# A decoder block on one Trainium2 core: the second delta-net chain keeps its convolved tiles in SBUF, reloads change queue, column sums and four x tiles are moved

## The chip, the cores and the metric

One core of one Trainium2 chip runs the whole block in one launch. The metric is the device time of that core in microseconds, the median over several runs. Engines are named as the profile does: PE (TensorE), DVE (VectorE), ACT (ScalarE), POOL (GpSimd) and SP (SyncE). SP, ACT and POOL can each start DMA transfers, and each does so from an in-order queue of its own instructions (SPq, ACTq, POOLq).

## The reference, cut to what matters

One layer on 512 tokens of width 2048, float32. A vector c gives six modulation rows through w_ada; two token mixers (latent attention and gated delta-net) read the same projection p; they are merged by sigmoid gates, and a SwiGLU mixer follows.

```python
mod = c_act @ w_ada[l] + b_ada[l]
sh_a, sc_a, gt_a, sh_f, sc_f, gt_f = [m[:, None, :] for m in jnp.split(mod, 6, axis=-1)]
h = _rmsnorm(x, norm_mix[l]) * (1.0 + sc_a) + sh_a
p = h @ w_in[l]
c_q, c_kv, k_pe, q_g, k_g, v_g, z, b_logit, a_logit, gate_logits = _split_cols(p)
y_a = _mla_branch(c_q, c_kv, k_pe, ...) @ w_o_mla[l]
qkv = jnp.concatenate([q_g, k_g, v_g], axis=-1)
y_b = _gdn_branch(qkv, z, b_logit, a_logit, ...) @ w_o_gdn[l]
g_a, g_b = jnp.split(jax.nn.sigmoid(gate_logits), 2, axis=-1)
mix = (g_a * y_a + g_b * y_b) @ w_o[l]
x = x + gt_a * mix
...
# _gdn_branch: 8 heads of 128
qkv = _causal_conv_silu(qkv, conv_w)        # width 4, along the tokens
q = _l2norm(q) * DK ** -0.5 ; k = _l2norm(k)
# _gated_delta_chunked, chunks of 64 tokens
A = Lmat + I                                # Lmat: strictly lower, k k^T with decay
u, w = triangular_solve(A, [v * beta, k * beta * exp(G)])
def step(S, inp):                           # scanned over the chunks
    v_new = u_c - w_c @ S
    o = (q_c * exp(G_c)) @ S + a_c @ v_new
    S = S * exp(G_last) + k_dec^T @ v_new
```

## The kernel before, in words

**Matmuls.** Each weight tile comes from HBM as float32 (`raw`, `raws`), is split into a rounded part `hi` (ACT) and a rest `lo` (DVE), and PE takes three products for one. A *unit* is 24 matmuls on 512 tokens, and PE runs the units of w_in, w_ukv, w_uq, w_o_mla, w_o_gdn, w_o, w_gate_up and w_down one behind the other. Stages are named by their PSUM tiles: v (551 to 612 us), gb0 to gb3 (the four groups of the second gate, 612 to 875), qpe, v0, v1, qk, ya, yb (1106 to 1193), then `m` of w_o in two halves of its width (1193 to 1270 and from there), and gate-up and down.

**Order.** The whole program is first recorded in a `Score`, then emitted. PE, POOL and SP keep the order in which the program recorded their instructions; for DVE and ACT a list scheduler (`Score.order`) chooses by due times. Generators (`Driver`) advance side work between the units: the delta-net chains, the attention, the column sums. All instructions are emitted in one place, so every row of the profile has the line L490; rows are told apart by tile names.

**SBUF.** 68 shared slots of 128 x 512 (`S(name)`) hold nearly every tile that lives for some time; 5 wide buffers hold raw weights. Weight loads are issued 4 ahead, splits 2 ahead.

**DMA helpers.** `load()` issues on SP, `side()` on POOL, `nc.scalar.dma_start` on ACT.

**The delta-net.** `conv_tile(idx, p)` convolves one of 24 tiles (idx 0 to 7 are the eight heads of q, 8 to 15 those of k, 16 to 23 those of v, in `cv_dram[0]` to `cv_dram[2]`; heads 0 to 3 of each belong to chain 0, 4 to 7 to chain 1), stores it in `cv_dram` and keeps some in `conv_out`. `gdn(g)` is a chain of four heads, g = 0 and 1: it turns q and k tiles on PE (`pq`, `pk`), builds L and the attention products, solves the triangular systems by blocks (`fsL`, `fsX` on DVE, stored in `fso`, reloaded as `T` tiles; `T64T`, `TT`, `M` join the blocks), and scans four chunks of 128 tokens with `vp`, `AT` and `kdec`, which it stored in `gdn_dram` and reloads by `back(c)`. `conv_back(j, g)` reloads four convolved tiles. `pause(ns)` holds a chain back until the planner's clock has moved so far.

**Column sums.** The modulation rows are sums over the rows of w_ada, and over w_in's gate columns for another term, in 160 *extras*: a 512-KB load and DVE work each (`rawm`, `rawa`). `PLAN` says how many extras go with a unit, by the unit's index: (n, r) means r per unit up to index n. Unit indexes: v stage 97 to 104, gb0 105 to 112, gb1 113 to 120, gb2 121 to 128, gb3 129 to 136, qpe 137 and 138, v0 and v1 139 to 142, qk 143 to 150, ya from 151, yb 171 to 190.

**w_o.** `X_AT` says before which unit (n, i) of w_o which x tiles (token tile, column tile) are loaded. In the second half, stored partial sums (`raws<-s_dram`) and a row of the gate (`row<-gm_dram`) are reloaded on the same SP queue; ACT's and DVE's `euvw` are combinations of weight tiles that PE's `m` takes as its operand.

Of the kernel before, what the change touches and what calls it, by code (L numbers as in the profile page):

```python
# [499 lines left out]
def block_kernel(ctx: ExitStack, tc: tile.TileContext, a: dict, out):  # L500
    score = Score(tc)
    nc = Core(score)
# [16 lines left out]
    def S(s, dt=F32):  # L519
        return slots.tile([P, 512], dt, tag="s", name=nm(s))  # L520
# [10 lines left out]
    def side(dst, src, **kw):  # L531
        nc.gpsimd.dma_start(dst, src, **kw)
# [3 lines left out]
    def tok(j):  # L536
        return slice(j * P, (j + 1) * P)
# [347 lines left out]
    conv_out = {}  # L885

    def conv_tile(idx, p):
        acc = S("cv")
        nc.scalar.activation(acc[:], p[:], AF.Copy, scale=cw[:, 72 + idx:73 + idx])
        for w in (2, 1, 0):  # L890
            sft = 3 - w
            nc.vector.scalar_tensor_tensor(acc[:, sft:], p[:, :T - sft], cw[:, 24 * w + idx:24 * w + idx + 1],
                                           acc[:, sft:], op0=ALU.mult, op1=ALU.add)
        nc.scalar.activation(acc[:], acc[:], AF.Silu)
        side(cv_dram[idx // 8, idx % 8], acc[:])
        conv_out[idx] = acc if idx in (0, 1, 2, 3, 8, 9, 10, 11) else None

    cv_dram = dram.tile([3, 8, P, 512], F32, name="cv_dram")

    def conv_back(j, g):  # L900
        res = []
        for i in range(4 * g, 4 * g + 4):
            x = S("cv")
            nc.scalar.dma_start(x[:], cv_dram[j, i])
            res.append(x)
        return res

# [8 lines left out]
    def conv_gen():  # L916
        while True:
            if conv_queue:
                conv_tile(*conv_queue.popleft())
            yield  # L920
# [165 lines left out]
    def pause(ns):  # L1086

        until_ = score.time + ns
        while score.time < until_:
            yield  # L1090

    gdn_dram = dram.tile([2, 3, NT, P, 512], F32, name="gdn_dram")
    mid = set()

    def gdn(g):
# [5 lines left out]
        def back(c):  # L1101
            res = []
            for j in (0, 1, 2) if c < NT - 1 else (0, 1):
                x = S(("vp", "AT", "kdec")[j])
                nc.scalar.dma_start(x[:], gdn_dram[g, j, c])
                res.append(x)
            return res

        def conved(*parts):
            while not all(8 * j + 4 * g + i in conv_out for j in parts for i in range(4)):  # L1110
                yield

        yield from conved(0, 1)
        while "eG" not in G or (g and "loops" not in mid):
            yield
        if g:
            kT, qT = conv_back(1, 1), conv_back(0, 1)
            yield 9
        else:
            qT, kT = ([conv_out.pop(b + i) for i in range(4)] for b in (0, 8))  # L1120
            yield 4
        yield from conved(2)
        while g and 0 not in mid:
            yield
        vT = conv_back(2, g)

        def tr4(src, c, name):
            ps = PS(name)
# [86 lines left out]
        for j in range(31):  # L1215
# [4 lines left out]
            nc.vector.tensor_tensor(fsX[:, j + 1:, 0:w], fsX[:, j + 1:, 0:w], tv, ALU.subtract)  # L1220
            if j % 8 == 7:
                yield
        yield from pause(34000.0)
        for hf in range(2):
            side(fso[g].rearrange("b c h i a -> (b c h) i a")[:, :, 16 * hf:16 * hf + 16], fsX[64 * hf:64 * hf + 64])
        del fsX_, fsX, fsT, fsL
# [2 lines left out]
        for b in range(4):  # L1229
            side(T32[32 * b:32 * b + 32, :].rearrange("p (n a) -> p n a", a=32),  # L1230
                                fso[g][b].rearrange("c h i a -> i (c h) a"))
        yield from pause(11000.0)
        while g and "second" not in mid:
            yield
        T64 = [S("T64"), S("T64")]
# [59 lines left out]
        while not (g or 1 in mid):  # L1295
            yield
        kT, qT, cur = conv_back(1, g), conv_back(0, g), back(0)
        yield 5
        for hf in range(2):
# [12 lines left out]
        for c in range(NT):  # L1312
# [3 lines left out]
            if c < NT - 1:  # L1316
                cur = back(c + 1)
# [458 lines left out]
    def mix_row(n):  # L1776
        g_mix[n] = S("row")
        load(g_mix[n][:], gm_dram[512 * n:512 * n + 512].partition_broadcast(P))

    def load_x(t, n, src):  # L1780
        x2[t, n] = S("x2")
        load(x2[t, n][:], src[:, 512 * n:512 * n + 512])
# [254 lines left out]
    def plan(i):  # L2037

        return next(r for n, r in PLAN if i < n)

    PLAN = ((17, 2.0), (33, 0.0), (89, 0.4), (97, 0.0), (113, 0.5), (137, 1.5), (143, 1.0), (156, 0.0), (175, 2.0), (1000, 1.5))

    cs_dram = dram.tile([D], F32, name="cs_dram")
    gparts = kpe[:, 0, :].rearrange("p (k j) -> p k j", j=4)
# [35 lines left out]
    def with_pre(units, fn):  # L2080
        u = units[0]
        p0 = u.pre

        def pre():
            fn()
            if p0 is not None:
                p0()
        u.pre = pre
        return units
# [137 lines left out]
    def mixing():  # L2227
# [73 lines left out]
        def start_gdn():  # L2301
            drv.ahead = LOADS
            for g in range(2):
                ch["AB"[g]] = drv.add(gdn(g))
                drv.add(gated_out(g))
# [43 lines left out]
        for n in range(4):  # L2349
            us = fm_set(f"yb{n}", lambda k0, nk, n=n: plain(w_og, k0, nk, 512 * n, 512), 512, 8, ov, yb_done(n))  # L2350
            if n == 0:
# [4 lines left out]
                with_pre(us, fin)  # L2356
            yield read_gates("b", n)
            yield from us
        X_AT = {(0, 12): ((0, 1),), (0, 14): ((1, 1),), (1, 0): ((2, 1),), (1, 1): ((3, 1), (0, 3)), (1, 2): ((0, 0), (1, 3)), (1, 3): ((1, 0), (0, 2)),
                (1, 4): ((2, 0), (1, 2)), (1, 5): ((3, 0), (2, 3)), (1, 6): ((3, 3),), (1, 7): ((2, 2), (3, 2))}  # L2360
        for n in range(2):
            us = tokens_wo(n)
            if n == 0:
# [9 lines left out]
            for i, u in enumerate(us):  # L2373
                if n == 0 and i in (12, 13):
                    with_pre([u], lambda i=i: mix_row(i - 12))
                if n and i in (4, 5):
                    with_pre([u], lambda i=i: mix_row(i - 2))
                if (n, i) in X_AT:
                    with_pre([u], lambda c=X_AT[n, i]: [load_x(t, f, a["x"][tok(t), :]) for t, f in c])
                if n and i == 16:  # L2380
# [878 lines left out]
    def everything():  # L3259
        yield from mixing()  # L3260
        yield from ffn()
# [58 lines left out]
```

## Time and profile before

| | |
|---|---|
| three runs | 2684.03, 2680.06, 2679.77 us, median 2680.06 |
| the profiled execution | 2676.04 us, its span 2674.3 us, mean granted clock 0.992 |
| busy time | PE 2642.3, DVE 2252.0, ACT 1298.1, POOL 250.0 us |
| moved by DMA | 649.00 MB, mean 243 GB/s |
| DMA issues from 600 to 900 us | `cv<-cv_dram` 28 on ACT, 256 KB, 5.4 us to landing; `vp` 8, `AT` 8, `kdec` 6 on ACT; `rawa` 32 and `raw` 27 on SP, 512 KB, 5.9 and 5.6 us |

The profile is one execution. A row of a timeline has the start, the duration, the engine or queue, the tiles written and read, and in brackets the time that the engine was idle before and what ended that. A row of the windows has each engine's busy time, then the granted TensorE clock as a share of full speed, then the DMA engines' mean busy share and the rate. A queue such as ACTq is the time that the engine's sequencer spends issuing transfers; while it does, later instructions of that engine stand behind.

### The profile page before, as it was taken

To read this page: it belongs to the slowest core of one execution; us is meant where nothing else is said; L and a number is where in the kernel's file an instruction comes from. 1 tells how busy PE (TensorE), PEld (TensorE's weight loads), DVE (VectorE), ACT (ScalarE), POOL (GpSimd) and SP (SyncE) were. 2 spreads that over 40 slices of the span, in tenths; PEclk is the share of its full clock that TensorE was granted. 3 is DMA by queue.
4 is the path that set the end of the run, shared out by engine and by line. 5 is a ranking of instruction groups with operands and counts; after the bars stand their busy time and mean duration, and the time that the engine had idled before them with its cause. 6 is when DMAs were issued, how large, how long until landed. Compare 5 with 4: busy or idle time off the path is not lost.

```text
span 2674.3 us, 36928 instructions
## 1 busy us (share of the span) xinstructions
PE 2642.3 (99%) x12652; PEld 2196.4 (82%) x12652; DVE 2252.0 (84%) x3447; ACT 1298.1 (49%) x2004; POOL 250.0 (9%) x427
## 2 busy tenths in 40 slices
PE   9999999999999999999999999999999999999998
PEld 7888888887787888888788888888888888888887
DVE  8988888888986878899897888888887888877888
ACT  4355444464444684235484444444444445444445
POOL 0000110132410000000100000000000001010000
PEclk9999999999998999999999999999999999999999
DMA  9985777886888738956864777776766668686785
GB/s 351 351 282 165 260 272 259 308 281 228 260 276 274 236 105 273 332 176 207 269 205 132 237 236 241 248 234 226 236 227 205 208 222 277 210 247 226 226 294 207
DMA packets 335540, 649.00 MB, mean 243 GB/s; under 512 B 48116, under 2 KB 77108, under 8 KB 335352
## 3 DMA queue, kind: packets, MB, share of 16 engines
q1 hardware_dynamic: 277624, 511.43, 58.0%
q0 software_dynamic: 29584, 94.18, 9.7%
q10 hardware_dynamic: 28144, 41.03, 4.5%
q8 instruction: 99, 1.62, 0.2%
q14 instruction: 89, 0.73, 0.1%
HBM read 537.95 MB, written 107.50 MB: 241 GB/s over the span
## 4 chain that ended last, share of the span: by engine, by line
PE 85%; DMA 6%; issue 4%; DVE 3%; ACT 1%; ACTq 0%; SPq 0%; POOL 0%; DVEq 0%; POOLq 0%
PE m L490 52%; PE v L490 4%; PE gu L490 3%; PE ya L490 3%; PE ga L490 3%; PE yb L490 3%; PE s L490 3%; PE gb L490 2%; PE dn L490 2%; PE qk L490 2%; PE dnt L490 2%; DMA rawa<-in_w_in_dram 1%; PE sc L490 1%; DMA raws<-in_w_down_dram 1%; DMA raw<-in_w_in_dram 1%
## 5 line engine op out<-in xcount | busy, mean ns | idle before, releaser
L490 ACT CAST hi<-raws 128x512 fp32r<-128x512 f32 (+1 forms) x472 | 430.5, 915 | 666.1 <-PE m L490 338.1
L490 DVE TENSOR_TENSOR lo<-raws,hi 128x512 fp32r<-128x512 f32 (+1 forms) x472 | 487.9, 1051 | 153.8 <-ACT hi L490 148.2
L490 ACT CAST hi<-raw 128x1024 fp32r<-128x1024 f32 (+2 forms) x183 | 185.0, 1014 | 257.9 <-DMA raw<-in_w_in_dram 93.7
L490 PE MATMUL m<-hi,xh 128*128 128x512 f32 x704 | 274.5, 390 | 1.6 <-ACT euvw L490 1.6
L490 PE MATMUL m<-lo,xh 128*128 128x512 f32 x704 | 274.4, 390 | 0.1
L490 PE MATMUL m<-hi,xl 128*128 128x512 f32 x704 | 274.4, 390 | 0.0
L490 DVE TENSOR_TENSOR lo<-raw,hi 128x1024 fp32r<-128x1024 f32 (+2 forms) x183 | 216.6, 1188 | 48.0 <-ACT hi L490 38.8
L490 ACT CAST hi<-sums 128x1024 fp32r<-128x1024 f32 x160 | 168.1, 1051 | 141.9 <-PE m L490 120.2
L490 DVE TENSOR_TENSOR lo<-sums,hi 128x1024 fp32r<-128x1024 f32 x160 | 195.3, 1221 | 36.5 <-ACT hi L490 36.0
L490 DVE TENSOR_TENSOR sums<-raws,raws 128x1024 f32<-128x1024 f32 x160 | 195.2, 1220 | 23.0 <-DMA raws<-in_w_down_dram 7.8
L490 POOL DMA_DIRECT2D s_dram<-raws x160 | 87.0, 544 | 1285.0 <-DVE raws L490 1253.2
L490 DVE CUSTOM_DVE_ANT_0 rawm<-rawm,cbc 128x1024 f32<-128x1024 f32 x160 | 195.2, 1237 | 13.8 <-DMA rawm<-in_w_mod_dram 13.4
L490 PE MATMUL m<-hi,h2h 128*128 128x512 f32 x480 | 188.7, 393 | 0.0
L490 PE MATMUL m<-hi,h2l 128*128 128x512 f32 x480 | 187.0, 389 | 0.0
L490 PE MATMUL m<-lo,h2h 128*128 128x512 f32 x480 | 186.8, 389 | 0.0
L490 PEld LDWEIGHTS m<-hi,xh 128*128 128x128 f32 x704 | 132.4, 188 | 29.8 <-ACT euvw L490 2.3
L490 PEld LDWEIGHTS m<-lo,xh 128*128 128x128 f32 x704 | 132.4, 188 | 27.9 <-DVE lo L490 0.5
L490 PEld LDWEIGHTS m<-hi,xl 128*128 128x128 f32 x704 | 132.5, 188 | 27.5
L490 DVE TENSOR_TENSOR raws<-raws,raws 128x512 f32<-128x512 f32 x160 | 108.0, 686 | 29.6 <-DMA raws<-in_w_gate_up_dram 8.6
L490 DVE TENSOR_TENSOR raws<-sums,raws 128x512 f32<-128x512 f32 x160 | 110.0, 688 | 2.2
L490 PE MATMUL gb<-hl,hi 128*128 128x512 f32 x256 | 106.2, 415 | 0.0
L490 PEld LDWEIGHTS m<-hi,h2l 128*128 128x128 f32 x480 | 90.1, 188 | 18.9
(543 smaller groups left out, 6352.6 us busy)
## 6 DMA issues: line engine op xcount, KB each, us to landing
raws<-in_w_gate_up_dram SPq DMA_DIRECT2D x400, 256.0 KB, 3.8
rawm<-in_w_mod_dram SPq DMA_DIRECT2D x160, 512.0 KB, 5.8
raws<-in_w_in_dram SPq DMA_DIRECT2D x160, 256.0 KB, 4.4
s_dram<-raws POOLq DMA_DIRECT2D x160, 256.0 KB, 3.8
raws<-s_dram SPq DMA_DIRECT2D x160, 256.0 KB, 3.9
raws<-in_w_down_dram SPq DMA_DIRECT2D x160, 256.0 KB, 4.9
raw<-in_w_in_dram SPq DMA_DIRECT2D x79, 512.0 KB, 5.8
raws<-in_w_o_dram SPq DMA_DIRECT2D x80, 256.0 KB, 4.2
```

The lines of the kernel that those rows point to most:

```text
L490: self.tc.keep_in_program_order(op.call(*op.args, **op.kwargs))
```

## The change

Four things are changed.

1. `conv_tile` keeps the tiles of chain 1 too (idx 4 to 7, 12 to 15, 20 to 23) in `conv_out`; 20 to 23 are no longer stored. `gdn(1)` takes its q, k and v from there and not by `conv_back`: 12 reloads of 256 KB and 4 stores less. The 12 slots are held for longer.
2. The scan's reloads (`back`, 22 in both chains) and the later `conv_back` reloads of q and k (16) are issued on POOL's queue instead of ACT's. The four v tiles of chain 0 stay on ACT's. The two pauses of a chain around the solve are 3 and 2 us longer in the planner's clock.
3. `PLAN` deals the column sums anew.
4. Four x tiles of w_o's second half are loaded up to nine units later.

```diff
-        conv_out[idx] = acc if idx in (0, 1, 2, 3, 8, 9, 10, 11) else None
+        if idx < 20:
+            side(cv_dram[idx // 8, idx % 8], acc[:])
+        conv_out[idx] = None if 15 < idx < 20 else acc
...
# conv_back(j, g)
-            nc.scalar.dma_start(x[:], cv_dram[j, i])
+            (nc.scalar.dma_start if j == 2 else side)(x[:], cv_dram[j, i])
...
# gdn(g), back(c)
-                nc.scalar.dma_start(x[:], gdn_dram[g, j, c])
+                side(x[:], gdn_dram[g, j, c])
...
-        if g:
-            kT, qT = conv_back(1, 1), conv_back(0, 1)
-            yield 9
-        else:
-            qT, kT = ([conv_out.pop(b + i) for i in range(4)] for b in (0, 8))
-            yield 4
+        qT, kT = ([conv_out.pop(b + 4 * g + i) for i in range(4)] for b in (0, 8))
+        yield 4
...
-        vT = conv_back(2, g)
+        vT = [conv_out.pop(20 + i) for i in range(4)] if g else conv_back(2, 0)
...
-        yield from pause(34000.0)
+        yield from pause(37000.0)
...
-        yield from pause(11000.0)
+        yield from pause(13000.0)
...
-    PLAN = ((17, 2.0), (33, 0.0), (89, 0.4), (97, 0.0), (113, 0.5), (137, 1.5), (143, 1.0), (156, 0.0), (175, 2.0), (1000, 1.5))
+    PLAN = ((17, 2.0), (33, 0.0), (89, 0.4), (97, 0.0), (105, 0.3), (113, 0.8), (129, 1.0), (143, 1.5), (151, 0.5), (156, 0.0), (175, 2.0), (1000, 1.3))
...
# X_AT, entries of the second half that differ
-        (1, 3): ((1, 0), (0, 2)), (1, 4): ((2, 0), (1, 2)), (1, 7): ((2, 2), (3, 2))
+        (1, 3): ((1, 0),), (1, 4): ((2, 0),), (1, 9): ((0, 2), (1, 2)), (1, 11): ((2, 2),), (1, 12): ((3, 2),)
```

How this moves instructions. First ACT in gb0, about 636 to 650 us, before (`fsd`, `fsL` belong to chain 0's solve, `hi` are weight splits):

```order
L490 CAST hi_1256<-raw_1222 128x1024
L490 DMA fsd_108<-LT_1230 32x4x32 x4
L490 CAST hi_1260<-raw_1242 128x1024
L490 DMA cv_1266<-cv_dram 128x512
L490 DMA cv_1267<-cv_dram 128x512
L490 DMA cv_1268<-cv_dram 128x512
L490 DMA cv_1269<-cv_dram 128x512
L490 DMA cv_1250<-cv_dram 128x512
L490 DMA cv_1251<-cv_dram 128x512
L490 CAST hi_1263<-raw_1245 128x1024
L490 DMA fsL_1236<-fsd_108 64x512 x2
L490 DMA fsL_1237<-fsd_108 64x512 x2
```

The same place of ACT after, with the Silu of the last convolved tiles (`cv_1246<-cv_1246` and its like):

```order
L490 ACTIVATE cv_1246<-cv_1246 128x512
L490 CAST hi_1248<-raw_1230 128x1024
L490 ACTIVATE cv_1247<-cv_1247 128x512
L490 DMA fsL_1236<-fsd_108 64x512 x2
L490 DMA fsL_1237<-fsd_108 64x512 x2
L490 ACTIVATE cv_1222<-cv_1222 128x512
L490 CAST hi_1252<-raw_1242 128x1024
L490 CAST hi_1271<-raw_1250 128x1024
```

The six reload issues between two splits are gone. Next POOL in gb2, about 759 to 773 us, before (`fso<-fsX` stores chain 0's solved blocks, `T<-fso` reloads them):

```order
L490 MEMSET TT_1399 64x4x64
L490 MEMSET TT_1400 64x4x64
L490 DMA fso_111<-fsX_1380 2048x1x16 x2
L490 DMA T_1343_1484<-fso_111 32x16x32 x4
L490 MEMSET T_1366_1507 128x512
L490 MEMSET T_1367_1508 128x512
L490 MEMSET T64T_1509 128x512
```

The same place of POOL after:

```order
L490 DMA vp_1414<-gdn_dram 128x512
L490 DMA AT_1415<-gdn_dram 128x512
L490 DMA kdec_1416<-gdn_dram 128x512
L490 DMA fso_111<-fsX_1350 2048x1x16 x2
L490 DMA vp_1432<-gdn_dram 128x512
L490 DMA AT_1433<-gdn_dram 128x512
L490 DMA kdec_1434<-gdn_dram 128x512
L490 DMA T_1300_1441<-fso_111 32x16x32 x4
L490 DMA vp_1446<-gdn_dram 128x512
L490 DMA AT_1447<-gdn_dram 128x512
L490 DMA kdec_1448<-gdn_dram 128x512
```

The chunks' reloads now stand before, between and behind the stores and reloads of the solve. Last SP in the second half of w_o, about 1290 to 1310 us, before:

```order
L490 DMA x_2351_2496<-in_x_dram 128x512
L490 DMA x_2352_2497<-in_x_dram 128x512
L490 DMA row_2498<-gm_dram 128x512
L490 DMA raws_2505<-in_w_o_dram 128x512 x2
L490 DMA raws_2506<-s_dram 128x512
L490 DMA x_2362_2507<-in_x_dram 128x512
L490 DMA x_2363_2508<-in_x_dram 128x512
L490 DMA row_2509<-gm_dram 128x512
L490 DMA raws_2515<-in_w_o_dram 128x512 x2
L490 DMA raws_2516<-s_dram 128x512
L490 DMA x_2372_2517<-in_x_dram 128x512
L490 DMA raws_2523<-in_w_o_dram 128x512 x2
```

The same place of SP after:

```order
L490 DMA x_2338_2483<-in_x_dram 128x512
L490 DMA row_2484<-gm_dram 128x512
L490 DMA raws_2491<-in_w_o_dram 128x512 x2
L490 DMA raws_2492<-s_dram 128x512
L490 DMA x_2348_2493<-in_x_dram 128x512
L490 DMA x_2349_2494<-in_x_dram 128x512
L490 DMA row_2495<-gm_dram 128x512
L490 DMA raws_2501<-in_w_o_dram 128x512 x2
L490 DMA raws_2502<-s_dram 128x512
L490 DMA x_2358_2503<-in_x_dram 128x512
L490 DMA raws_2509<-in_w_o_dram 128x512 x2
```

One of two x tiles ahead of the first row is gone; the like holds one unit earlier, and the two that stood a unit later come behind this piece.

More of the change, by code (lines that the diff above doesn't have):

```diff
@@ L894, in conv_tile @@
         nc.scalar.activation(acc[:], acc[:], AF.Silu)
-        side(cv_dram[idx // 8, idx % 8], acc[:])
-        conv_out[idx] = acc if idx in (0, 1, 2, 3, 8, 9, 10, 11) else None
+        if idx < 20:
+            side(cv_dram[idx // 8, idx % 8], acc[:])
+        conv_out[idx] = None if 15 < idx < 20 else acc
     cv_dram = dram.tile([3, 8, P, 512], F32, name="cv_dram")
@@ L2358, in mixing @@
             yield from us
-        X_AT = {(0, 12): ((0, 1),), (0, 14): ((1, 1),), (1, 0): ((2, 1),), (1, 1): ((3, 1), (0, 3)), (1, 2): ((0, 0), (1, 3)), (1, 3): ((1, 0), (0, 2)),
-                (1, 4): ((2, 0), (1, 2)), (1, 5): ((3, 0), (2, 3)), (1, 6): ((3, 3),), (1, 7): ((2, 2), (3, 2))}
+        X_AT = {(0, 12): ((0, 1),), (0, 14): ((1, 1),), (1, 0): ((2, 1),), (1, 1): ((3, 1), (0, 3)), (1, 2): ((0, 0), (1, 3)), (1, 3): ((1, 0),),
+                (1, 4): ((2, 0),), (1, 5): ((3, 0), (2, 3)), (1, 6): ((3, 3),), (1, 9): ((0, 2), (1, 2)), (1, 11): ((2, 2),),
+                (1, 12): ((3, 2),)}
         for n in range(2):
```

## The prediction

> **What bounds the kernel now.** I read the page's head first, then TensorE's busy time in 10-us windows, then its waits, then the queues behind the waits. The first fence is the page's rows for span and busy time.
>
> ```profile
> span 2674.3 us, 36928 instructions
> PE 2642.3 (99%) x12652; PEld 2196.4 (82%) x12652; DVE 2252.0 (84%) x3447; ACT 1298.1 (49%) x2004; POOL 250.0 (9%) x427
> ```
>
> TensorE bounds it: 32 us of 2674 are idle, so no change outside TensorE can gain more than these, plus what the lowered clock costs after each gap. The windows show where that lies. Columns: window; length; busy time of PE, PE's weight loads, DVE, ACT, POOL; granted clock; DMA share; GB/s.
>
> ```profile
> 640.00:650.00 10.00, 8.01 (x36) 6.25 (x35) 1.81 (x6) 1.04 (x1) 0.00 (x0) 1.00 1.04 385
> 650.00:660.00 10.00, 7.23 (x30) 6.13 (x31) 7.38 (x18) 3.36 (x18) 0.54 (x1) 0.66 0.82 257
> 670.00:680.00 10.00, 9.27 (x44) 7.36 (x43) 9.76 (x41) 6.12 (x8) 0.01 (x1) 1.00 0.48 161
> 700.00:710.00 10.00, 9.07 (x107) 7.37 (x106) 9.93 (x17) 1.65 (x2) 6.29 (x9) 1.00 0.88 286
> 730.00:740.00 10.00, 8.85 (x56) 7.19 (x55) 8.67 (x27) 7.57 (x12) 0.00 (x0) 0.83 0.76 250
> 810.00:820.00 10.00, 8.32 (x170) 6.87 (x156) 3.24 (x6) 1.16 (x3) 0.00 (x0) 1.00 1.02 368
> 820.00:830.00 10.00, 9.03 (x41) 7.41 (x40) 9.47 (x26) 4.00 (x8) 0.00 (x0) 0.66 1.02 365
> 830.00:840.00 10.00, 9.73 (x67) 8.00 (x65) 5.54 (x20) 7.12 (x17) 0.00 (x0) 1.00 0.70 248
> 840.00:850.00 10.00, 7.54 (x24) 5.99 (x25) 8.41 (x20) 4.76 (x7) 0.00 (x0) 0.56 0.97 284
> 850.00:860.00 10.00, 10.00 (x55) 8.59 (x55) 2.55 (x4) 3.02 (x8) 0.00 (x0) 0.92 0.79 229
> 1090.00:1100.00 10.00, 10.00 (x50) 8.37 (x49) 6.88 (x9) 3.26 (x4) 0.00 (x0) 1.00 0.97 342
> 1310.00:1320.00 10.00, 6.60 (x23) 4.60 (x22) 6.13 (x9) 5.36 (x8) 0.00 (x0) 0.79 1.01 365
> 1320.00:1330.00 10.00, 10.00 (x40) 8.12 (x40) 8.23 (x11) 4.55 (x6) 0.00 (x0) 0.87 0.68 243
> ```
>
> What a place costs is taken as idle time (10 less PE's busy time) plus busy time × (1 − clock). Place A (640 to 660): 1.99 + 2.77 idle, 7.23 × 0.34 = 2.5 clock, 7.2 us. Place B (670, 700, 730): 0.73 + 0.93 + 1.15 idle, 8.85 × 0.17 = 1.5 clock, 4.3 us. Place C (810 to 860): 1.68 + 0.97 + 0.27 + 2.46 idle, 3.1 + 3.3 + 0.8 clock, 12.6 us. Place E (1310 to 1330): 3.4 idle, 1.4 + 1.3 clock, 6.1 us. Together 30 us. A and C have the DMA engines full (share about 1.0, 365 to 385 GB/s), but so has 1090 to 1100 (0.97), where PE does not stall: a full DMA stalls only where something urgent stands late in it. The waits say what was urgent (us in total, times, longest).
>
> ```profile
> PE pk L490 <- DMA cv<-cv_dram: 4.8, 2, 3.3
> PE m L490 <- ACT euvw L490: 3.4, 2, 1.8
> PE cT L490 <- ACT ckv L490: 2.3, 1, 2.3
> PE M L490 <- issue: 1.7, 1, 1.7
> ```
>
> **Part 1: the second chain's tiles stay in SBUF, 12 reloads and 4 stores fewer.** Place A in the timeline, ACT's queue and engine, then PE (start, us, instruction, idle time before and its releaser):
>
> ```profile
> 636.85 10.72 ACTq L490 DMA_DIRECT2D cv<-cv_dram  x6
> 647.61 1.04 ACT L490 CAST hi<-raw 128x1024 fp32r<-128x1024 f32 x1 [10.13 <-DMA cv<-cv_dram]
> 652.77 0.47 PE L490 MATMUL pk<-kc,cv 128*128 128x128 f32 x1 [3.29 <-DMA cv<-cv_dram]
> ```
>
> Six reload issues hold ACT's in-order queue for 10.7 us; the weight split (hi<-raw) behind them comes 10 us late, and PE's pk, which turns the reloaded tiles, waits 4.8 us in two pieces. In the changed order these issues are not there (the excerpt in the section on the change), and pk reads tiles that ScalarE's Silu wrote in SBUF. Both causes leave. Late next is the split itself, whose raw tile must land through the same DMA, now with 8 reloads (2.1 MB, 5.4 us at 385 GB/s) less ahead of it. At best A's 7.2 us go, at worst the raw tile is late by as much and nothing goes; the rows lie nearer the first, since the load that stalls is itself removed. I take −6.
>
> The price: 12 of 68 shared slots are held from the convolution to the chain's use. Any load that waits for a slot then goes out later. No row shows a slot wait by that name. A count of the free-slot order in the changed program gives weights 12.6 us or more of matmul time between issue and first use in the 660-to-680 stretch (13.6 at the shortest before), and 20 to 41 us from 730 on. Bounds: 0, and what a late weight load costs, A again, +7.2. I take +1.5, put under B, since a landing of 5.9 us, as in this row of the DMA issues (KB each, us to landing), fits in 12.6 us twice.
>
> ```profile
> rawm<-in_w_mod_dram SPq DMA_DIRECT2D x12, 512.0 KB, 5.9
> ```
>
> **Part 2: 38 reloads go from ACT's queue to GpSimd's.** Place C is where the second chain's v tiles and the scan's reloads meet the solve's copies on ACT. ACT and its queue, then PE:
>
> ```profile
> 813.22 1.81 ACTq L490 DMA_DIRECT2D cv<-cv_dram  x2
> 818.64 0.38 ACT L490 ACTIVATE T<-X 32x256 f32<-32x256 f32 x1 [7.90 <-DMA cv<-cv_dram]
> 827.68 0.58 ACT L490 COPY M<-M 64x512 f32<-64x512 f32 x1 [4.32 <-DMA cv<-cv_dram]
> 819.11 1.11 PE L490 MATMUL M<-T,LT 64*64 64x64 f32 x16 [1.68 <-issue]
> 842.04 3.17 PE L490 MATMUL cT<-kc,ckv 128*128 128x128 f32 x8 [2.31 <-ACT ckv L490]
> ```
>
> ACT's T copy waits 7.9 us behind reload issues and PE's M follows it (0.47 us later by start; "issue" in PE's row is the same wait seen through its sequencer). The v reloads go altogether, the others to a queue that does nothing else there: POOL is busy 0.00 us in all five windows from 810 to 860. Of C's price, M's first pair of gaps (1.68 + 0.97, with the 0.66 clock's 3.1) is 5.8 us and this cause leaves entirely. The cT gap (2.31, with 3.3 + 0.8 clock, 6.4 us) waits for ckv, which stays on ACT's queue and comes out of the same full DMA. By a count of the bytes in the two orders, 7.6 MB less have been asked for by 800 than before, while the stretch from 800 to 870 asks for the same rate as before. So the backlog that made 1.02 is gone at its start, but not the rate. Bounds for C: 0 and −12.6; I take −5 for M and −2 for cT, −7.
>
> What the new queue costs. Issues: 38 × 0.56 us = 21 us of POOL (row below), which is 9% busy; nothing on PE's path is computed there after 710 but the solve's stores. A wait: the scan's reloads now stand in one in-order queue with fso<-fsX, which waits for DVE's solve, and T<-fso, which waits for that store to land.
>
> ```profile
> 598.37 0.56 POOL L490 DMA_DIRECT2D gdn_dram<-vp  x1
> 758.57 0.18 DVE L490 TENSOR_TENSOR fsX<-fsX,fsT 128x16 f32<-128x16 f32 x1
> 759.29 2.18 POOL L490 DMA_DIRECT2D fso<-fsX  x2 [41.30 <-issue]
> 768.62 2.59 POOL L490 DMA_DIRECT2D T<-fso  x4 [7.16 <-PE pqs L490]
> 734.49 0.45 ACTq L490 DMA_DIRECT2D vp<-gdn_dram  x1
> ```
>
> ```profile
> vp<-gdn_dram ACTq DMA_DIRECT2D x8, 256.0 KB, 4.8
> gdn_dram<-vp POOLq DMA_DIRECT2D x6, 256.0 KB, 4.6
> ```
>
> Before, vp went out at 734 whatever the solve did. After, the second chunk's vp, AT and kdec go out behind fso, the third's behind T<-fso. In the changed order they have 13.7 and 14.8 us of matmuls between issue and first use (counted at 0.22 us each, 36 in 8.01 us in the window at 640). With 4.8 us to land, 9 us of slack remain, so I cost the wait at 0; the cover is that the solve's end at 758.57 does not slip by 9 us against PE. Bounds: 0, and the 7.2 us of POOL's own wait in each chain (a rival below). An issue on POOL's queue took 0.56 us at 598 while DVE was busy 10 us of 10 (window, third time column), and landings are 4.6 us there against 4.8 on ACT's:
>
> ```profile
> 590.00:600.00 10.00, 10.00 (x64) 8.86 (x63) 10.00 (x13) 3.11 (x4) 8.20 (x8) 1.00 0.85 266
> ```
>
> One rule speaks against this part. The Trainium skill, SBUF — State Buffer, section "SBUF: two separate sides", says that descriptors of a GpSimd-issued DMA are written by GpSimd's own cores, which a VectorE instruction holding the shared port pair locks out, and that the ACT or SP queue is the cure. By its figure (620 ns become about 3100, in the section on the bandwidth-pool intuition) a triple of reloads would land an estimated 7.5 us later, and the rival below would begin after 1.5 us of slip. The trace does not bear that out, by the 0.56 and 4.6 us just shown; the sum by that rule is the rival's 2685, by the rows my forecast.
>
> **Part 3: the deal of column sums.** Each is a 512-KB load and about 1.24 us of DVE, by its group on the page:
>
> ```profile
> L490 DVE CUSTOM_DVE_ANT_0 rawm<-rawm,cbc 128x1024 f32<-128x1024 f32 x160 | 195.2, 1237 | 13.8 <-DMA rawm<-in_w_mod_dram 13.4
> ```
>
>  Units (24 matmuls, 5.4 us): the stage after 551 gets 2.4 instead of 4, gb0 (612 to 668) 6.4 instead of 4, gb1 and gb2 16 instead of 24, gb3 12 as before, qpe, v0 and v1 9 instead of 6, qk 4 instead of 0; the sum is 49.8 against 50, so DVE and DMA do the same work in all. Some 4 MB move from 670–800 to 875–1000. That is the 700 and 730 windows' relief, while gb0's DVE gets 2.4 × 1.24 = 3 us more in 56. Against it, the deal lets weights of gb1's first units come at 300 to 460 GB/s by the count of bytes, over the 385 that was reached. For B I take −1 for the relief (its releasers are DVE, POOL and ACT, and none is moved far), which with +1.5 from above makes +0.5; bounds −4.3 and +7.2. The tail, 1.3 instead of 1.5 from unit 175 on, I cost at nothing: at 1090, in the stretch just ahead, the DMA is full and so is PE.
>
> **Part 4: four x tiles of w_o come later.** Place E: a reload of stored partial sums is awaited by DVE, behind it ACT's euvw and PE's m (the last row is of the chain of waits: start, us).
>
> ```profile
> 1313.87 0.69 DVE L490 TENSOR_TENSOR raws<-raws,raws 128x512 f32<-128x512 f32 x1 [4.23 <-DMA raws<-s_dram]
> 1302.76 0.94 SPq L490 DMA_DIRECT2D raws<-s_dram  x1
> 1302.76 11.02 DMA raws<-s_dram
> ```
>
> 256 KB take 11 us to land. On SP's queue two x tiles stand less ahead of it (0.5 MB, 1.4 us at 365 GB/s), and two that were issued behind it move away too, which share the engines while it lands (another 1.4 us at most). DVE's 4.23 us then become 1.4 to 2.8, and PE's 3.4 us of waits mostly close. Bounds 0 and −6.1; I take −4. The tiles' new place is 23 us or more ahead of their use, against landings of 11 at the worst, so they cost nothing there.
>
> **Sum.** −6 (A) + 0.5 (B) − 7 (C) − 4 (E) = −16.5. The profiled execution took 2676.0 us (span 2674.3 and 1.7 around it), 4.0 under the runs' median of 2680.06. From the one 2659.5 would follow, from the other 2663.6; I state the second, since the measure is the median.
>
> **Rivals.** *The gain is given back* (no change): by the count, the same bytes still cross 800 to 870, and the loads at 670 are bunched. If C keeps its 12.6, B gets A's price again at +7.2 and E halves (−3), the sum is −7.2 (A) + 7.2 − 3 = −3, 2677. For it: windows at 1.02 share with the clock at 0.66. Against: the rows of C name ACT's queue. *POOL's queue becomes the wait* (slower): if the solve's end slips by over 9 us against PE, PE's scan products wait in both chains. At the 7.2 us that POOL waited for T<-fso, a wait of that length in each chain, with the clock's loss on top as at A (7.2 in all for 4.8 of wait, ×1.5), costs 2 × 10.8 = 21.6, less 16.5: +5, 2685. At 12 us of wait in each it is 2700. It decides from 5.5 us a chain (16.5 / 3). Against it: 9 us of slack by rows. *All places close*: −28 to −30, 2651, if cT's backlog is gone too.
>
> **Chances.** Forecast (2656 to 2674) 0.56; all places close 0.15; given back (2674 to 2685) 0.17; POOL's queue or bunched weights, slower, 0.12. 0.2% is 5.4 us, about what a measurement here can tell from no change: faster is under 2674.7, slower over 2685.4. So faster 0.72, same 0.16, slower 0.12. The range, 2648 to 2683, leaves out the slower case and a little of the same.
>
> **What would show it.** A: no wait of pk for cv, 640 to 660 with PE at 10 and clock 1.00. C: no T<-X copy waiting for a cv reload; if cT still waits for ckv at a DMA share of 1.0, that −2 was wrong. Part 2: kdec, AT and vp on POOL's queue landing within 6 us and no PE wait on them; if PE's scan products wait for these reloads, I am wrong on the sign. Slots: PE waits on hi or lo at 668 to 700. E: the last reload of stored sums lands in under 9 us. I am wrong if gaps of about 5 us open in gb1 or gb3 that the trace of before doesn't have.

## The result, and the profile after

The changed kernel takes 2667.72 us (median of four runs, 2665.24 to 2670.12) against 2680.38 us (four runs, 2679.77 to 2684.03): 12.7 us less, a ratio of 0.995 with a 95% interval of 0.9933 to 0.9967. The forecast was 2663.6 us, −16.5, with 2648 to 2683 as its range. The profiled execution has a span of 2663.4 us, 10.9 less than before. The page's first rows, after:

```profile
span 2663.4 us, 36957 instructions
PE 2634.1 (99%) x12652; PEld 2189.3 (82%) x12652; DVE 2250.9 (85%) x3447; ACT 1309.3 (49%) x2013; POOL 269.4 (10%) x461
```

Two corrections to the section on the change. The four x tiles are loaded four to six units later, not up to nine. And the `fso<-fsX` at 759 us in its excerpt of POOL before is the second chain's store; the first chain's went out at 685.96.

The 10-us windows at the places of the prediction (same columns as there), after:

```profile
640.00:650.00 10.00, 10.00 (x62) 8.65 (x60) 9.31 (x25) 7.85 (x47) 1.09 (x2) 1.00 0.23 85
650.00:660.00 10.00, 10.00 (x45) 8.24 (x45) 9.76 (x18) 4.25 (x23) 3.15 (x3) 1.00 0.26 79
660.00:670.00 10.00, 9.02 (x50) 7.56 (x50) 9.83 (x44) 6.45 (x9) 1.12 (x2) 1.00 0.11 39
730.00:740.00 10.00, 8.68 (x54) 6.94 (x54) 9.39 (x23) 6.00 (x11) 0.54 (x1) 0.83 0.35 114
760.00:770.00 10.00, 8.12 (x52) 7.03 (x51) 7.87 (x17) 3.73 (x13) 6.83 (x13) 1.00 1.05 351
800.00:810.00 10.00, 9.25 (x163) 7.23 (x161) 0.92 (x5) 1.81 (x9) 2.08 (x4) 1.00 1.04 402
810.00:820.00 10.00, 7.28 (x42) 6.21 (x43) 8.35 (x26) 7.05 (x14) 1.72 (x4) 0.67 0.90 316
...
840.00:850.00 10.00, 10.00 (x70) 9.19 (x69) 8.32 (x20) 4.63 (x15) 0.00 (x0) 1.00 0.97 316
1300.00:1310.00 10.00, 7.40 (x31) 5.47 (x31) 7.41 (x10) 4.98 (x8) 0.00 (x0) 1.00 1.00 352
```

Place A (640 to 660) is full, and its DMA share fell from 1.04 to 0.23. The gap at 840 and its 0.56 clock are gone, but one at 810 with 0.67 stands in C, and 730 lost as much as before. PE's waits, after (us in total, times, longest):

```profile
PE M L490 <- ACT T L490: 4.8, 3, 1.8
...
PE m L490 <- ACT euvw L490: 2.6, 2, 2.2
PE pks L490 <- DVE Sst L490: 1.9, 1, 1.9
PE gb L490 <- ACT cp L490: 1.5, 1, 1.5
...
PE pv L490 <- ACT cv L490: 1.0, 1, 1.0
```

No wait for a reload of cv is left. The largest is now M for the solve's T copies on ACT, which was 1.0 us in one piece by that name before, and 1.7 more under `issue` if that is read as the prediction did. The 1.0 us of pv is new: the Silu of the tiles that now stay in SBUF comes a little late. ACT's timeline at C, a line of the chain of waits there, and PE's timeline show where it comes from:

```profile
796.77 6.79 ACTq L490 DMA_DIRECT2D gb_dram<-sg  x4
...
808.19 0.31 ACT L490 ACTIVATE sq<-o 128x128 f32<-128x128 f32 x1 [10.94 <-DMA gb_dram<-sg]
...
810.43 0.38 ACT L490 ACTIVATE T<-X 32x256 f32<-32x256 f32 x1
```

```profile
796.77 11.44 DMA gb_dram<-sg
```

```profile
810.95 1.11 PE L490 MATMUL M<-T,LT 64*64 64x64 f32 x16 [1.70 <-ACT T L490]
813.83 1.94 PE L490 MATMUL M<-T,LT 64*64 64x64 f32 x16 [1.77 <-ACT T L490]
```

With the DMA engines full (1.04), four stores of the gate stretch over 6.8 us in ACT's in-order queue, ACT stands 10.9 us, and the T copies come behind. The row of 6.79 us is not 6.8 us of issuing: its four issues took 0.83, 0.69, 0.40 and 0.33 us, and the rest lies between them. By the chain of waits, what ended ACT's 10.9 us is the landing of one of these stores, after 11.4 us: `sq` reads nothing of that store, so it probably waited for the shared slot that the store frees, which was not traced. The prediction's row of 10.72 us at A is of the same kind: its six issues took 0.33 to 1.59 us each, 3.4 us together. The reloads have left ACT's queue; what stays there meets the same full DMA. Before, the row of this step named reloads of cv and 7.9 us.

The table adds, over windows, PE's idle time and busy time × (1 − clock), as the prediction did. Each row is one profiled execution; the first 600 us and the end are not in it.

| | 600–640 | 640–690 (A) | 690–790 (B) | 790–880 (C) | 1290–1350 (E) |
|---|---|---|---|---|---|
| before | 0.6 | 7.9 | 3.7 | 12.6 | 6.1 |
| after | 1.5 | 1.1 | 4.7 | 6.6 | 2.8 |

A −6.8, B with the stretch ahead of it (600 to 640) +1.9, C −6.0, E −3.3: −14.2. Over all windows from the start on it is −12.6, mostly since the first 600 us lost 2.0 more. By place the forecast (−6, +0.5, −7, −4) was close. The runs below show that by part it was not. Nor was it by kind: of C's −6.0 only 1.3 is idle time of PE (5.4 before, 4.1 after) and 4.7 clock, and of E's −3.3 only 0.6 is idle time (3.4 and 2.8) and 2.7 clock.

### The profile page after: what moved, and what is told of

The parts are those of the page before. It is cut to its first block, busy times and chain, and to the rows that moved or that the text cites. A ratio compares the mean times of both kernels' runs of the same rounds, so it can differ in the third digit from the quotient of the medians.

```text
span 2663.4 us, 36957 instructions
## 1 busy us (share of the span) xinstructions
PE 2634.1 (99%) x12652; PEld 2189.3 (82%) x12652; DVE 2250.9 (85%) x3447; ACT 1309.3 (49%) x2013; POOL 269.4 (10%) x461
## 4 chain that ended last, share of the span: by engine, by line
PE 87%; DVE 5%; DMA 4%; ACT 3%; issue 1%; SPq 0%; ACTq 0%; DVEq 0%
PE m L490 56%; PE v L490 4%; PE gu L490 3%; PE ga L490 3%; PE yb L490 3%; PE ya L490 3%; PE s L490 3%; PE gb L490 2%; PE dn L490 2%; PE dnt L490 2%; DVE lo L490 1%; PE qk L490 1%; DMA raw<-in_w_in_dram 1%; DMA raws<-in_w_down_dram 1%; PE aT L490 1%
## 5 line engine op out<-in xcount | busy, mean ns | idle before, releaser
L490 PEld LDWEIGHTS m<-lo,h2h 128*128 128x128 f32 x480 | 90.2, 188 | 18.1
```

Of the source, the lines that this page charges most:

```text
L490: self.tc.keep_in_program_order(op.call(*op.args, **op.kwargs))
```

## The experiments

The parts were first run alone on the kernel before, then undone one at a time in the changed kernel. Then part 2 was taken apart. A shift in us is the ratio applied to 2680.

| kernel | median us | before, same chip | ratio, 95% interval | shift |
|---|---|---|---|---|
| the change | 2667.7 | 2680.4 | 0.9950, 0.9933–0.9967 | −13 |
| part 1 alone | 2662.6 | 2678.7 | 0.9940, 0.9927–0.9952 | −16 |
| part 2 alone | 2675.0 | 2678.7 | 0.9986, 0.9977–0.9995 | −4 |
| part 3 alone | 2669.8 | 2678.7 | 0.9964, 0.9951–0.9976 | −10 |
| part 4 alone | 2679.1 | 2678.7 | 1.0001, 0.9992–1.0010 | 0 |
| part 1 undone | 2671.1 | 2680.0 | 0.9967, 0.9955–0.9979 | −9 |
| part 2 undone | 2657.0 | 2680.0 | 0.9919, 0.9905–0.9932 | −22 |
| part 3 undone | 2665.5 | 2680.0 | 0.9948, 0.9936–0.9960 | −14 |
| part 4 undone | 2669.1 | 2680.0 | 0.9957, 0.9944–0.9970 | −12 |
| reloads on ACT, long pauses kept | 2671.1 | 2679.2 | 0.9973, 0.9963–0.9983 | −7 |
| q and k reloads on ACT | 2664.8 | 2679.2 | 0.9953, 0.9941–0.9965 | −13 |
| scan reloads on ACT | 2667.2 | 2679.2 | 0.9955, 0.9944–0.9967 | −12 |
| q and k reloads spread on POOL | 2666.8 | 2679.2 | 0.9951, 0.9938–0.9964 | −13 |

**Part 1 alone: tiles stay in SBUF.**

```diff
-        side(cv_dram[idx // 8, idx % 8], acc[:])
-        conv_out[idx] = acc if idx in (0, 1, 2, 3, 8, 9, 10, 11) else None
+        if idx < 20:
+            side(cv_dram[idx // 8, idx % 8], acc[:])
+        conv_out[idx] = None if 15 < idx < 20 else acc
...
+        qT, kT = ([conv_out.pop(b + 4 * g + i) for i in range(4)] for b in (0, 8))
+        yield 4
...
-        vT = conv_back(2, g)
+        vT = [conv_out.pop(20 + i) for i in range(4)] if g else conv_back(2, 0)
```

> The kernel before with part 1 alone (chain 1's convolved tiles stay in SBUF; the other reloads on ACT's queue, the old deal, the old x places). Theory (each part pays at its own place): A's wait of pk for cv goes and 640 to 660 is full, 6 to 7 us; C loses the v reloads ahead of the T copies and so 2 to 4 us; total -8 to -11 against the kernel before. Rival 1 (the new deal of column sums pays, by taking bytes off gb1 to gb3): under -3. Rival 2 (the queue change pays, since ACT's copies stay behind the other reloads): A goes, C stays at 12 us, -6 to -7.

Measured −16, more than the theory's −8 to −11. The whole change gave −13; the two intervals overlap (0.9927–0.9952 and 0.9933–0.9967). Its windows, and its wait in C:

```profile
640.00:650.00 10.00, 10.00 (x61) 8.56 (x59) 9.31 (x25) 7.72 (x50) 1.09 (x2) 1.00 0.21 81
650.00:660.00 10.00, 10.00 (x46) 8.25 (x45) 9.72 (x18) 4.54 (x21) 3.25 (x3) 1.00 0.25 79
820.00:830.00 10.00, 5.09 (x23) 3.88 (x21) 4.17 (x14) 5.21 (x12) 0.00 (x0) 1.00 1.00 351
```

```profile
PE py L490 <- issue: 6.1, 1, 6.1
```

A is full without any other part. C still costs 9.7 us in this profile (12.6 before), as one wait of the scan's py. The profile's sums give 13.0 us (36.2 before, 23.2 here): A 6.8, B with the stretch ahead of it 3.2, C 2.9, E 1.1, less small gaps ahead of 600 us. So B is the term that I had not given to this part. C's 2.9 us are clock alone: PE's idle time there is 6.7 us against 5.4.

**Part 2 alone: the queue, with the pauses.**

```diff
-            nc.scalar.dma_start(x[:], cv_dram[j, i])
+            (nc.scalar.dma_start if j == 2 else side)(x[:], cv_dram[j, i])
...
-                nc.scalar.dma_start(x[:], gdn_dram[g, j, c])
+                side(x[:], gdn_dram[g, j, c])
...
-        yield from pause(34000.0)
+        yield from pause(37000.0)
...
-        yield from pause(11000.0)
+        yield from pause(13000.0)
```

> The kernel before with part 2 alone (38 later reloads and the 8 q and k reloads of chain 1's start by POOL's queue, v reloads on ACT's, the two longer pauses). Theory: ACT's weight split at 636 is no longer behind six reload issues, but pk still waits for the reloaded tiles, so A keeps 3 to 5 of 7.2 us; C's M gap shrinks by 2 to 4; total -3 to -7. Rival 2 (the queue change is what pays): -8 or more. Rival 3 (GpSimd's queue delays the reloads: fso and T stand ahead of them): +2 or more.

Measured −4, in the theory's band. Its profile is of an execution of 2679.0 us, 4 over the median, and shows A at 8.7 us and C at 9.2. A did not shrink as that theory said: pk and pq wait 5.9 us for the reloaded tiles, where pk waited 4.8 before.

**Part 3 alone: the deal.** The edit is the `PLAN` line of the diff.

> The kernel before with part 3 alone (the new deal). Theory: -2 to +3, since A has more loads at gb0 and C the same rate as before; A's wait grows. Rival 1 (the deal pays): -5 or more, with C's 12.6 us at half.

Measured −10: the rival's side. In its profile C costs 3.8 us (12.6 before), A 4.8 (7.9) and B 1.5 (3.7). Two of its C windows:

```profile
810.00:820.00 10.00, 10.00 (x68) 8.30 (x67) 6.74 (x16) 5.33 (x10) 0.00 (x0) 1.00 1.03 378
820.00:830.00 10.00, 10.00 (x54) 8.19 (x53) 8.14 (x26) 9.35 (x23) 0.00 (x0) 1.00 1.05 365
```

The DMA share is as full as before (1.03 and 1.05), and PE does not stall there now. So the deal does not pay by emptying the DMA in these two windows. That it pays by changing which transfers are late is what remains, and is not shown. The byte count was right that the DMA stays full there, and wrong to conclude that it costs the same.

**Part 4 alone: the x tiles.** The edit is the `X_AT` entries of the diff.

> The kernel before with part 4 alone (four x tiles of w_o later). Theory: only 1300 to 1330 changes; the 6.1 us there become 2 to 3, total -3 to -4. Rival (the stored sums' reload is late for the weights' traffic and not for the x tiles): 0 to -1, the 11-us landing stays.

Measured 0, within 2.7 us either way: the rival. The windows of E, and DVE's wait there:

```profile
1310.00:1320.00 10.00, 8.38 (x38) 6.63 (x37) 4.56 (x7) 4.07 (x7) 0.54 (x1) 1.00 1.02 361
1320.00:1330.00 10.00, 7.85 (x27) 6.03 (x27) 10.00 (x16) 5.53 (x9) 0.00 (x0) 0.83 0.81 292
```

```profile
1316.98 0.69 DVE L490 TENSOR_TENSOR raws<-raws,raws 128x512 f32<-128x512 f32 x1 [5.44 <-DMA raws<-s_dram]
```

DVE still waits, 5.4 us against 4.2, and E costs 5.1 us against 6.1.

**The parts undone, one at a time.** Each takes the changed kernel and turns one of these diffs round.

> The changed kernel with part 1 undone (12 reloads and 4 stores back; q and k reloads on POOL's queue, v's on ACT's). Theory: A's wait for cv is back, +5 to +10 against the changed kernel, so -3 to -8 against the kernel before. Rival 1 (the deal pays): within 3 us of the changed kernel, -10 against before.

Part 1 undone: −9, so 4 to 5 us worse than the change, just short of the theory's 5 to 10; the two intervals overlap (0.9955–0.9979 and 0.9933–0.9967). A's waits for cv are back, in five pieces and not in two; here are two of them on PE:

```profile
651.81 0.33 PE L490 MATMUL pk<-kc,cv 128*128 128x128 f32 x1 [0.81 <-DMA cv<-cv_dram]
...
653.63 0.30 PE L490 MATMUL pq<-kc,cv 128*128 128x128 f32 x1 [1.49 <-DMA cv<-cv_dram]
```

A costs 11.5 us in this profile, but C nothing (0.0). The scan ends 14 us later there (its last pks at 889.6 us, 875.6 in the changed kernel) and PE does not stall at the later place, though the DMA share is 1.05 to 1.09 from 810 to 850. Why it does not stall there stays open.

> The changed kernel with part 2 undone (the later reloads on ACT's queue again, the old pauses). Theory: C is worse by 2 to 4 us, -9 to -11 against before. Rival 2 (the queue change is what pays): -5 or less against before. Rival 3 (GpSimd's queue costs something by its slower landings, 7 us against 4.8): faster than the changed kernel, -13 to -16 against before.

Part 2 undone: −22, the fastest median of this study, about 8 us under the changed kernel, with intervals that just do not touch (0.9905–0.9932 and 0.9933–0.9967). From part 1 alone (0.9927–0.9952) it is not told apart. The third expectation had the sign and neither the size nor, by the next run, the reason. Part 2 was not worth −5; beside the other three parts it cost about 8 us.

> The changed kernel with part 3 undone (the old deal). Theory: within 3 us of the changed kernel, -10 to -15 against before; with 1.5 sums per unit in gb1 and gb2 the 730 to 770 gaps grow and the 610 gap shrinks. Rival 1 (the deal pays): -7 or less against before.

Part 3 undone: −14, as the changed kernel. The deal is worth 10 us alone and nothing that these runs can tell beside the other three parts.

> The changed kernel with part 4 undone (four x tiles early again). Theory: +3 to +4 against the changed kernel, -9 against before, the wait for the stored sums at 1300 back to 4 us with PE idle for 3 to 4 us. Rival: no difference, since in the changed kernel DVE still waits 4 us there.

Part 4 undone: −12, not told apart from the changed kernel. E costs 2.9 us in its profile, the changed kernel 2.8. So E's fall is not the x tiles' doing. Each of the other three parts undone also left E at 1.8 to 2.4, and each alone at 4.8 to 7.4, so no single part is it either. What fell is mostly clock (2.7 of 3.3 us); what moves E stays open.

**Which half of part 2 costs.** My theory at this point was that GpSimd's queue issues the reloads early and bunched (eight in 4.3 us at 705.7), ahead of weights that are due sooner. The reloads went back to ACT, first all with the longer pauses kept, then one kind at a time, then spread on POOL:

```diff
# reloads on ACT, pauses of the change: both lines of the queue
-            (nc.scalar.dma_start if j == 2 else side)(x[:], cv_dram[j, i])
+            nc.scalar.dma_start(x[:], cv_dram[j, i])
...
-                side(x[:], gdn_dram[g, j, c])
+                nc.scalar.dma_start(x[:], gdn_dram[g, j, c])
```

> The changed kernel with its 38 reloads on ACT's queue again, but the longer pauses kept. It separates the two halves of part 2, which together cost about 8 to 10 us. Theory now (GpSimd's queue sends the reloads early and bunched, ahead of weights that are due sooner): the loss lies with the queue, so -20 to -24 against the kernel before, as with both undone. Rival (the longer pauses put the solve's copies where PE waits for them, M for T): -11 to -15, as the changed kernel.

Measured −7. The theory falls: with the long pauses, ACT's queue is no better than GpSimd's (−7 against −13, and their intervals overlap by 0.0004 only). Between this kernel and "part 2 undone" stand only the pauses, 37000 against 34000 and 13000 against 11000, and they cost 22 − 7 = 15 us, with intervals far apart (0.9905–0.9932 and 0.9963–0.9983). First the three windows of the kernel with short pauses, then those with long ones:

```profile
700.00:760.00 60.00, 60.00 (x519) 50.46 (x518) 53.76 (x122) 24.75 (x49) 9.42 (x19) 1.00 0.87 286
760.00:820.00 60.00, 59.99 (x537) 51.04 (x536) 47.52 (x116) 31.84 (x89) 4.37 (x10) 1.00 0.97 324
820.00:870.00 50.00, 48.07 (x301) 42.40 (x300) 40.55 (x91) 35.66 (x95) 0.00 (x0) 1.00 0.91 291
```

```profile
700.00:760.00 60.00, 60.00 (x506) 50.01 (x505) 51.17 (x113) 22.91 (x40) 7.84 (x15) 1.00 0.84 264
760.00:820.00 60.00, 57.84 (x515) 49.20 (x514) 49.71 (x128) 33.16 (x95) 6.96 (x14) 1.00 0.90 301
820.00:870.00 50.00, 43.41 (x261) 37.46 (x260) 27.35 (x61) 26.00 (x69) 0.00 (x0) 0.90 0.74 238
```

Up to 760 both are full. From there the long pauses lose 2.2 us, and then 6.6 with the clock at 0.90, where the short ones lose 1.9. POOL's store of the first chain's solve goes out 8.5 us later (677.55 and 686.08), that of the second chain's 4.7 us later, short pauses first:

```profile
748.55 2.17 POOL L490 DMA_DIRECT2D fso<-fsX  x2 [43.74 <-DVE fsX L490]
```

```profile
753.29 2.17 POOL L490 DMA_DIRECT2D fso<-fsX  x2 [47.11 <-DVE fsX L490]
```

The last pks products of the second scan stand 20 us later (877.9 against 857.4). With the long pauses PE's longest wait from 600 to 900 is there, and behind it a reload in ACT's queue:

```profile
PE pS L490 <- ACT yd L490: 4.3, 1, 4.3
```

```profile
ACT yd L490 <- DMA vp<-gdn_dram: 6.8, 1, 6.8
```

So both chains run later, and one wait behind a reload, 4.3 us, is the largest piece of what is lost. Why the later place is the worse one is not shown: the mean DMA share is lower with the long pauses in both stretches (0.90 and 0.74, against 0.97 and 0.91), so the DMA is not fuller on the whole.

> The changed kernel with the 16 q and k reloads on ACT's queue and the 22 of the scan (vp, AT, kdec) on GpSimd's. Theory (the bunch of eight q and k reloads does the harm): most of the loss is back, -18 to -23 against the kernel before, raw weights land sooner at 710 to 730. Rival (the scan's reloads stand behind fso and T in one in-order queue): -11 to -14, no better than the changed kernel.

> The changed kernel with the 22 reloads of the scan on ACT's queue and the 16 q and k reloads on GpSimd's. Theory: -12 to -16 against the kernel before, the bunch at 705 and 790 still there. Rival (in-order queue behind fso and T): -19 to -23.

> The changed kernel, all reloads on GpSimd's queue, but the eight q and k reloads of a chain are recorded behind the scan's first three and one or two at a step, over seven steps, instead of eight at once. Theory (bunching ahead of nearer weights): -16 to -22 against the kernel before. Rival (what counts is that GpSimd issues them at all: slower landing, 7 us against 5): -11 to -14, as the changed kernel.

The last of these is this edit. It also puts the scan's first three reloads ahead of the eight, where they stood behind them:

```diff
-        kT, qT, cur = conv_back(1, g), conv_back(0, g), back(0)
-        yield 5
+        cur, kT, qT = back(0), [], []
...
+        for _ in range(4):
+            one(1, kT)
+            yield
+        one(0, qT)
+        one(0, qT)
+        yield
...
+        one(0, qT)
+        one(0, qT)
         yield 3
```

Measured −13, −12 and −13: neither kind of reload, nor the bunch, makes a difference that these runs tell from the changed kernel. With the pauses of the change, all five ways of issuing lie at −7 to −13. GpSimd's queue with the short pauses was not run, so whether the queue move helps or harms there is open; that the 22 us need ACT's queue is not shown. Nor were the pauses run alone on the kernel before.

## Why the prediction was right, and where not

*The sum* was right in sign and size (−16.5 against −12.7), the time 4 us over the forecast and inside the range. That the size came out is in good part luck. A is the one place where the mechanism held; elsewhere two errors of opposite sign met. Parts 1, 3 and 4 together gave −22, where the sum has −9.5 for them (A, B and E), and part 2 on top of them cost about 8, where the sum has −7 (C).

*A, −6:* right, in mechanism and size. pk's wait is gone, 640 to 660 has PE at 10.00 and the clock at 1.00, as the prediction asked, and part 1 alone does it.

*B, +0.5:* near by number (+1.0 from 690 to 790), and by luck. The price put on the held slots did not show: part 1 alone took this stretch from 3.7 to 1.1 us. In the changed kernel B is 4.7, from M's wait for T and pks' for Sst; with part 2 undone it is 0.0, with only the pauses kept 2.2. Behind pks' 1.9 us the chain of waits has a late weight after all:

```profile
757.01 6.50 DMA raw<-in_w_in_dram
```

Its split ends on DVE at 765.8, and the copy of Sst stands behind it there. With part 2 undone this wait is not there, so the slots of part 1 alone do not make it.

*C, −7, given to the queue:* near in size by luck, wrong in cause. Alone, part 2 took 3.4 us off C in its profile; beside the other parts, C is 6.6 with it and 1.9 without it. The tiles alone take 2.9 off C, the deal alone 8.8, so the −6.0 measured are likely what these leave after the pauses took some back. The step that failed is the reading of ACT's row, "7.9 <- DMA cv", as a property of the reloads: with those gone from ACT's queue, ACT stood 10.9 us for a store of the gate. What stood next in that queue waited in the same full DMA (share 1.04). And with the reloads back on ACT's queue and the short pauses, C costs 1.9 us only, so the reloads in that queue need not cost.

*The pauses:* not costed at all. The diff's two lines, which I listed in the change and left out of the sum, are the largest single cost that the runs found, 15 us with the reloads on ACT's queue. That is the missing term, which the sum put at nothing without a reason.

*The deal, part of B:* mis-sized, −10 alone where I had −1 for it, and nothing more that the runs can tell beside the other parts.

*E, −4, given to the x tiles:* wrong. The reload's landing fell from 11.0 to 8.3 us in the chain of waits, under the 9 us given as the sign, and yet DVE waits about as long as before (3.98 and 4.23 us):

```profile
1302.59 0.69 DVE L490 TENSOR_TENSOR raws<-raws,raws 128x512 f32<-128x512 f32 x1 [3.98 <-DMA raws<-s_dram]
```

```profile
1294.26 8.31 DMA raws<-s_dram
```

By both runs on it, the tiles' worth cannot be told from 0. The sign was no test of the gain.

*GpSimd's queue as a wait (the rival on the slower side):* not seen. POOL waited for the solve 20.7 us ahead of fso, as foreseen, but no scan product of PE waited for vp, AT or kdec in the changed kernel. POOL did stand elsewhere: 6.6 us ahead of a kdec reload at 730.96, until a store of the gate had landed. Their landings, from the DMA issues of 600 to 900, changed kernel:

```profile
vp<-gdn_dram POOLq DMA_DIRECT2D x8, 256.0 KB, 7.0
AT<-gdn_dram POOLq DMA_DIRECT2D x8, 256.0 KB, 7.0
...
kdec<-gdn_dram POOLq DMA_DIRECT2D x6, 256.0 KB, 7.3
```

They are 2 to 4 us later than on ACT's queue before (4.8, 3.9 and 3.3), over the 6 us that I gave as the mark. The Trainium skill, SBUF — State Buffer, section "SBUF: two separate sides", has VectorE, while it runs an instruction in a two-port mode, lock GpSimd out of writing descriptors; 2 us and more of delay is of the size of its figure (620 ns become about 3100, so about 2.5 us). But other queues' transfers were slower too (the gate's stores on ACT 6.0 us against 4.2), each issue on POOL took about 0.54 us (0.56 in the prediction's row), and no run here separates the two. By the times, with the same pauses, issuing on POOL was not slower than on ACT.

*The parts do not add:* alone they give −16, −4, −10 and 0, together −13. Their profiles show them at the same few places, A, B and C, and what one has repaired another cannot.

## What to carry to other kernels

Price every line of a diff, a pause of a few microseconds in a planner's clock too: it moves a whole chain, and here it outweighed the queue change that it came with. Where several parts aim at the same stalls, run each alone and each undone; here the shifts alone added up to −30 for a change of −13, and only undoing found the part that costs. A row such as "ACT waits for DMA x" in a stretch with full DMA names who stood first in the queue, not what to remove; ask who stands there next. And a merged row of issues is not the time of issuing: look at the single issues before blaming them.

The version to keep is the change without its second part: 2657.0 us, ratio 0.9919 (0.9905 to 0.9932). Part 1 alone, a much smaller edit, is not clearly slower.

## What the runs showed of the hardware

The granted clock did not follow from the length of PE's gaps, in the changed kernel. One of 1.88 us left it at 1.00 (the window at 760), one of 1.32 us at 730 gave 0.83, and two of 1.70 and 1.77 us, 1.1 us of small matmuls apart, gave 0.67 at 810. The two that lost clock have the solve's 64x64 M products around the gap; PE's timeline at 730, after:

```profile
731.29 1.14 PE L490 MATMUL M<-T,LT 64*64 64x64 f32 x16
733.75 1.11 PE L490 MATMUL M<-T,LT 64*64 64x64 f32 x16 [1.32 <-ACT T L490]
734.80 0.69 PE L490 MATMUL gb<-hl,hi 128*128 128x512 f32 x1
```

From 731.29 to 734.80, 3.5 us, no full product ran, and the next one took 0.69 us where they take 0.39. Whether the small products count as idle there was not tried. A stall is priced by its own window, not by its length; and since most of what C and E gave back is clock, a forecast of their idle time alone would have missed it.
